# A second block of seven products per MLP, a new order of its groups, and weight loads split whole

## The chip, the cores and the metric

The kernel runs on one core of a Trainium2 chip. The metric is the device time of one execution in microseconds (us), the median of several runs; a profile is one more execution of the same program with the hardware profiler on.

The names used below: TensorE (PE, with its weight loads PEld) multiplies, VectorE (DVE) and ScalarE (ACT) work on tiles, GpSimd (POOL) does little here, and SyncE (SP) issues nearly all the transfers. Each engine takes its own instructions strictly in order and waits on semaphores for those of the others.

## The reference, cut to what matters

The input is 256 tokens by 1024 channels, in float32, and there are two layers. Each has a token mixer and then an MLP:

```python
def _conv_ffn(xn, w_up, conv_w, conv_b, w_down):      # D_FF = 2816
    a, gval = jnp.split(xn @ w_up, 2, axis=-1)
    a = depthwise_conv_of_width_3(a, conv_w) + conv_b
    return (jax.nn.gelu(a) * gval) @ w_down

for layer in range(2):
    h = h + _token_mixer(_rmsnorm(h, norm1[layer]), ...)   # w_in, pooling, attention with rel_bias, w_o
    h = h + _conv_ffn(_rmsnorm(h, norm2[layer]), ...)
return _rmsnorm(h, norm_f)
```

The attention adds to its scores a bias per head that depends on the distance of two tokens.

## The kernel before, in words

**Loads and pieces.** Every weight is read as float32 in loads of 1 MB (128 partitions of 2048 columns), into three buffers called raw. TensorE multiplies in a shorter format, so each weight is split into a high part wh, a cast by ScalarE (L259), and a low part wl, the rest raw - wh, by VectorE (L261). A product is then three passes: wh by the high part of the activations, wl by the high part, wh by the low part. A load is split in two pieces of 1024 columns, each with its own cast and difference, into five buffers for wh and five for wl. `W.get` (class Weights) is called when TensorE's matmuls of a piece are written down, and writes down the splits of the pieces up to four further on; so the order of the program is also the order of the splits on ScalarE and VectorE. A piece that comes free lets a later split begin, and a raw buffer that comes free lets SP issue a later load.

**Steps between the splits.** Other work of VectorE and ScalarE is put between the cast and the difference of a split (the list `W.between`), or behind a piece's matmuls.

**The MLP's up projection.** It is made in groups of 512 columns: ("a", n) of the branch a, ("g", n) of the branch gval, for n from 0 to 4, and ("b", 20), 256 columns of either. A group is two loads, four pieces of 12 matmuls each (`by_tokens`, L798), with tokens on the partitions. A group's sums go to channels on the partitions by a crossing: VectorE transposes (L852) two banks into a tile called crossing, SP writes 512 KB of it to memory (L857), and SP reads it back in four transfers of 128 KB (L864) into zg, zga or zb. These reads are held back until SP has issued the next load (`bring_back`), and they wait for the write to land.

**A block of seven products.** ("w", 3) makes the groups a3 and g3 together. The four quadrants 11, 12, 21, 22 of both groups' weights, and seven sums of them, are multiplied as in Strassen's method: 11, T1, 22, T2, 21, T3, T4, where the T's are sums of quadrants made by VectorE in the raw tiles (L344). Each is two half products of 6 matmuls (`products`, L917). The two plain groups would need 16 half products, the block needs 14. Copies by ScalarE (L1681, L1685, L1688) and adds by VectorE (L1692) bring the seven sums together: a "kept" sum for a, the banks p and q for g. Both go through a crossing. The attention part has one more block of this kind in each layer, for the values (the table VALUES).

**Pairs of steps.** The activated columns are made in eleven pairs (`steps_up`, f = 0, 2, ... 20). Each pair is: six fetches by ScalarE (L1602, L1604), two neighbour adds by VectorE (L1608, L1609), the gelu by ScalarE (L1612), the gate by VectorE (L1616), the cast actq by ScalarE (L1624) and the difference actk by VectorE (L1625). The table PAIR_PLACES says at which place each happens: a place is one piece or half product of the MLP, numbered from 4 pieces a group, and `at_place` (L1640) puts a pair's neighbours and gate between the splits of its place, and the fetch, gelu and the two keeps behind it.

**The down projection.** ("d", 8) and so on are the groups of w_down's rows (`residual_mm`, L715 to L717), of which the first pieces stand between the half products of the block (the "d" in the table BLOCK).

**The bias.** bt holds the bias of four heads, read once by five transfers on SP (L559).

Of the kernel before, what the change touches and what calls it, by code (L numbers as in the profile page):

```python
# [47 lines left out]
PAIR_PLACES = (  # L48
    (11, 14), (14, 16), (19, 22), (21, 23), (46, 48), (49, 51), (52, 54), (55, 57), (60, 62), (63, 65), (58, 60),
# [3 lines left out]
    ("11", 0), ("11", 1), "d", ("T1", 0), ("T1", 1), "d", "d", ("22", 0), ("22", 1), "d", ("T2", 0), ("T2", 1), "d",  # L53
    ("21", 0), ("21", 1), "d", ("T3", 0), ("T3", 1), "d", "d", ("T4", 0), ("T4", 1),
# [64 lines left out]
class Weights:  # L119
# [6 lines left out]
    RAW, BUFS, LOOK = 3, 5, 3  # L126

    def __init__(self, tc, pool, idle, small):
        self.tc, self.nc, self.pool, self.idle, self.small = tc, tc.nc, pool, idle, small
        self.loads, self.pieces = [], []  # L130
        self.n_loaded, self.n_split, self.n_got = 0, 0, 0
        self.raw, self.split = {}, {}
        self.live = set()
        self.behind, self.later = (), []
        self.last, self.rests = [None, None], {}
        self.between = []
# [3 lines left out]
        self.sums = {}  # L140

    def add(self, src, shape, cuts, tag=None):

        n = len(self.loads)
        self.loads.append((src, shape, tag))
        return [(n, cut, c_shape) for cut, c_shape in cuts]
# [61 lines left out]
    def _split(self, upto):  # L208
        nc = self.nc
        first = self.n_split  # L210
        while self.n_split < len(self.pieces):
            i = self.n_split
            n, cut, shape, slot = self.pieces[i]
            if i >= upto and (slot is None or i >= max(upto, first + 2) or i >= upto + 4 or i < 4):
                break
            if slot is None and len(self.live) == self.BUFS:
                break
            self.load(n + 1)
            with ExitStack() as queued:
                for insts, some in self.later:  # L220
                    for inst in insts if i in some else ():
                        if not self.by_hand:
                            queued.enter_context(self.tc.issue_after(inst.ins))
                for hi, lo, *_ in self.open_next():
                    hi()
                    self.run_between()
                    lo()
                if i in self.sums:
                    self.sums.pop(i)()
            self.load(self.ahead(i))  # L230

    def run_between(self):

        while self.between:
            self.between.pop(0)()

    def open_next(self):
# [3 lines left out]
        n, cut, shape, slot = self.pieces[i]  # L241
        if slot is None:
            self.live.add(i)
            h, l = (
                self.pool.tile([P, *shape], F32R, tag=tag, bufs=self.BUFS, name=f"{tag}{i}")
                for tag in ("wh", "wl")
            )
# [44 lines left out]
    def free(self, i):  # L292
        self.live.discard(i)


@with_exitstack
def encoder(ctx, tc, x, w_in, w_pool, pool_scale, w_a, w_b, w_o, norm1, norm2, w_up, conv_w,
# [32 lines left out]
    def use_block(units, made, first):  # L330
# [9 lines left out]
        def sum_later(i, name, j):  # L340

            def make():
                one, other = terms[name]
                nc.vector.tensor_sub(out=raw(name, j), in0=raw(one, j), in1=raw(other, j))  # L344

            W.sums[i] = make

        for j in range(2):
            sum_later(len(W.pieces) + first + j, "T1", j)
        behind = [u for u in units if len(u) > 2]  # L350
        for unit in units:
            if len(unit) > 2:
                W.use([unit])
                behind = behind[1:] or behind
                continue
            name, j = unit
            if name in SUMS:
                sum_later(len(W.pieces), SUMS[name], j)
            if name in ("22", "21"):
                W.use([made[name][j]])  # L360
            else:
                W.use([(behind[0][0], lambda t, name=name, j=j: raw(name, j), (2, 512))])

    def first_quadrants(w, n):
        return {
            "11": quadrant(w, 0, DFF + n * 512, "ybig"), "12": quadrant(w, 0, n * 512, "at2"),
        }

    def block(w, down, n, made):
        made = dict(made)  # L370
        d = rows(down, 0) + rows(down, 2 * P)
        made["22"] = quadrant(w, 1, n * 512)
        d += rows(down, 4 * P)
        made["21"] = quadrant(w, 1, DFF + n * 512)
        d += rows(down, 6 * P)
        d = iter(d)
        use_block([next(d) if unit == "d" else unit for unit in BLOCK], made, -2)
# [36 lines left out]
    for l in range(DEPTH):  # L414
# [24 lines left out]
        for kind, n in MLP_GROUPS:  # L439
            if (kind, n) == ("a", 2):  # L440
                corner = first_quadrants(w_up[l], 3)
            if kind == "w":
                block(w_up[l], w_down[l], n, corner)
            elif kind == "b":
                for j in range(2):
                    W.use(of_both(w_up[l], j * 512, n * P))
            elif kind == "d":
                for f in range(n, min(n + 4, NF), 2):
                    W.use(rows(w_down[l], f * P))
            else:  # L450
                for j in range(2):
                    W.use(rows(w_up[l], j * 512, 4, (kind == "g") * DFF + n * 512, 512))
# [74 lines left out]
    bt = const.tile([P, HPG, NT * P], F32, name="bt")  # L527

    def build_bias():
# [25 lines left out]
        nc.sync.dma_start(out=fd[0].rearrange("(h e) -> h e", h=HPG), in_=fsb)  # L555
        yield
        for blk, kind in enumerate((4, 3, 1, 0, 2)):
            src = bass.AP(fd.tensor, fd.offset + kind * 256, [[1, P], [NT * 256, HPG], [1, P]])
            nc.sync.dma_start(out=bt[:, :, blk * P : (blk + 1) * P], in_=src)  # L559
        yield  # L560

    def bias_of(t, hh):

        b = bt[:, hh]
# [556 lines left out]
    for l in range(DEPTH):  # L1121
# [203 lines left out]
        if l == 0:  # L1325
            visits["u", 1, 0] = visits["u", 1, 2] = ((next, bias),)

# [76 lines left out]
        def keep_gated(n):  # L1404
# [14 lines left out]
            4: ((W.bring_back,), (scores, 1)),  # L1419
# [21 lines left out]
        with tc.manual_schedule():  # L1441
# [16 lines left out]
            for kind, n in GROUPS:  # L1458
                if l and (kind, n) not in VALUES and not z_of.get(("k", 2)):
                    kz, q = keys_and_queries()  # L1460
                ps = None
                for unit in VALUES.get((kind, n), range(4)) if l else range(4):
                    if not isinstance(unit, int):
                        name, j = unit
                        products_of(name, j)
                        if j:
                            W.between.append(after[name])
# [77 lines left out]
        run(attended)  # L1545


        g1 = gain(norm1[l + 1] if l + 1 < DEPTH else norm_f)
# [82 lines left out]
        between, behind = {}, {}  # L1631
# [8 lines left out]
        def at_place(p, make, *first):  # L1640
            W.between = [*first, *(step for _, _, step in sorted(between.pop(p, ()), key=lambda x: x[:2]))]
# [24 lines left out]
        def block_units(n):  # L1666
# [3 lines left out]
                x2, s_of_x, lambda: mmp.tile([P, 512], F32, tag="mm", name="t_ps")  # L1670
            )

# [10 lines left out]
            def keep_fifth():  # L1683
                kept["m"] = big.tile([P, 2, 512], F32, tag="gates", name="kept")
# [10 lines left out]
            after = {  # L1695
                "11": (keep_first,), "T1": (keep_fifth,), "22": (keep_both,), "T2": (lambda: add(0),),
                "T3": (lambda: add(1),), "T4": (lambda: turn("g", 0, bank("p")), lambda: turn("g", 1, bank("q"))),
            }
            for unit in BLOCK:
                if unit == "d":  # L1700
                    yield lambda: next(down), ()
                else:
                    name, j = unit
                    yield lambda: products(name, j), after.get(name, ()) if j else ()
        with tc.manual_schedule():
            W.by_hand = 1
            place, turn = 8, ()
            for kind, n in MLP_GROUPS[1:]:
                ps = None
                if kind == "w":  # L1710
                    for make, after in block_units(n):
                        at_place(place, make, *turn)
                        place, turn = place + 1, after
                    continue
                for i in range(4):
                    if not between and not behind:
                        break
                    if kind == "d":
                        at_place(place, lambda: next(down), *turn)
                    else:  # L1720
                        ps = at_place(place, lambda: by_tokens(x2, 4, ps=ps, begin=i, end=i + 1), *turn)
                    turn = ()
                    place += 1
                if kind != "d":
                    turn = (lambda ps=ps, kind=kind, n=n: to_z(ps, kind, n),)
# [41 lines left out]
```

## Time and profile before

| | |
|---|---|
| time, median of 3 runs | 847.55 us (847.19 to 847.85) |
| the profiled execution | 848.11 us, of which the span is 846.3 us |
| granted TensorE clock, mean | 0.999 |
| ScalarE busy | 531.1 us, 63% of the span |
| share of the chain that ended last: PE, DMA, DVE, ACT | 90%, 3%, 3%, 2% |
| bytes moved | 214.02 MB, mean 253 GB/s |
| casts of 128x1024 by ScalarE (L259, wh) | 292, mean 1048 ns |
| differences of 128x1024 by VectorE (L261, wl) | 292, mean 1219 ns |

The first lines of a profile's page give busy time of each engine. A table of windows gives it for a stretch of the span. A timeline gives single instructions, as start, duration, engine, line and operation, tiles, and in brackets the idle time before it and who ended it. Waits are by engine: who waited, for which instruction, how long in all, how often, and the longest.

### The profile page before, as it was taken

How to read it: one execution, taken by the hardware profiler on the slowest of the kernel's cores; microseconds unless marked ns; L12 is line 12 of the kernel's file. 1: busy time of each engine (PE TensorE's matmuls, PEld its weight loads, DVE VectorE, ACT ScalarE, POOL GpSimd, SP SyncE). 2: the span in 40 equal slices, each digit the busy share in tenths (PEclk: the TensorE clock that was granted, in tenths of full speed). 3: DMA queues.
4: the chain of work that ended last, by engine and by line, in shares of the span. 5: the costliest groups of instructions: out<-in, count | busy, mean ns of one | idle time of the engine just before them, and what ended most of it. 6: DMA issues, size and time to landing. Idle time of an engine off the chain costs nothing.

```text
span 846.3 us, 10959 instructions
## 1 busy us (share of the span) xinstructions
PE 838.7 (99%) x3889; PEld 699.3 (83%) x3889; DVE 665.5 (79%) x860; ACT 531.1 (63%) x770; POOL 35.5 (4%) x96
## 2 busy tenths in 40 slices
PE   9999999999999999999999999999999999999997
PEld 7888888888888887888888888888888888888886
DVE  6968877757767799788898997868577867998884
ACT  7744556655554776488765555577455647757883
POOL 1720000000010000000000000000000100000000
PEclk9999999999999999999999999999999999999999
DMA  8699987796759886889857669968777499768861
GB/s 305 211 304 289 317 282 251 246 282 218 233 206 302 276 275 199 256 264 316 272 185 225 222 225 316 284 235 261 247 261 269 164 308 309 227 224 275 303 218 50
DMA packets 147967, 214.02 MB, mean 253 GB/s; under 512 B 7801, under 2 KB 69185, under 8 KB 147913
## 3 DMA queue, kind: packets, MB, share of 16 engines
q1 hardware_dynamic: 147480, 212.67, 76.8%
q10 hardware_dynamic: 432, 0.66, 0.2%
q8 instruction: 30, 0.49, 0.2%
q14 instruction: 25, 0.20, 0.1%
HBM read 186.02 MB, written 27.28 MB: 252 GB/s over the span
## 4 chain that ended last, share of the span: by engine, by line
PE 90%; DMA 3%; DVE 3%; ACT 2%; issue 1%; POOL 0%; ACTq 0%; SPq 0%; DVEq 0%; POOLq 0%
PE t_ps L798 54%; PE res_ps L716 6%; PE res_ps L715 6%; PE res_ps L717 6%; PE t_ps L917 4%; PE v_ps L798 3%; DMA raw<-in_w_up_dram 3%; PE v_ps L1101 3%; PE v_ps L917 2%; PE pool_ps L702 1%; PE v_ps L1000 1%; PE o_ps L1392 1%; PE s_ps L1344 1%; ACT wh L259 1%; DVE wl L261 1%; PE s_ps L1339 1%
## 5 line engine op out<-in xcount | busy, mean ns | idle before, releaser
L261 DVE TENSOR_TENSOR wl<-raw,wh 128x1024 fp32r<-128x1024 f32 x292 | 350.9, 1219 | 92.4 <-ACT wh L259 91.7
L798 PE MATMUL t_ps<-wh,x 128*128 128x512 f32 x1280 | 401.8, 390 | 0.0
L259 ACT CAST wh<-raw 128x1024 fp32r<-128x1024 f32 x292 | 302.1, 1048 | 158.8 <-PE t_ps L798 71.2
L798 PEld LDWEIGHTS t_ps<-wh,x 128*128 128x128 f32 x1280 | 240.3, 188 | 50.0
L798 PE MATMUL t_ps<-wl,x 128*128 128x512 f32 x640 | 249.0, 389 | 0.0
L798 PEld LDWEIGHTS t_ps<-wl,x 128*128 128x128 f32 x640 | 120.2, 188 | 24.7
L715 PE MATMUL res_ps<-wh,actq 128*128 128x512 f32 (+1 forms) x184 | 70.0, 380 | 0.0
L716 PE MATMUL res_ps<-wl,actq 128*128 128x512 f32 (+1 forms) x184 | 69.8, 380 | 0.0
L717 PE MATMUL res_ps<-wh,actk 128*128 128x512 f32 (+1 forms) x184 | 69.3, 380 | 0.0
L798 PE MATMUL t_ps<-wh,po 128*128 128x512 f32 x128 | 41.4, 395 | 0.0
L715 PEld LDWEIGHTS res_ps<-wh,actq 128*128 128x128 f32 x184 | 34.6, 188 | 6.7
L716 PEld LDWEIGHTS res_ps<-wl,actq 128*128 128x128 f32 x184 | 34.6, 188 | 6.7
L717 PEld LDWEIGHTS res_ps<-wh,actk 128*128 128x128 f32 x184 | 34.6, 188 | 6.5
L1604 ACT ACTIVATE a<-zga,prm 128x256 f32<-128x256 f32 x80 | 38.9, 512 | 0.0
L592 POOL TENSOR_SCALAR ss<-ss 128x1 f32<-128x1 f32 x8 | 3.1, 386 | 764.2 <-ACT junk L585 764.2
L344 DVE TENSOR_TENSOR raw<-raw,raw 128x1024 f32<-128x1024 f32 x24 | 29.3, 1222 | 0.0
L798 PEld LDWEIGHTS t_ps<-wh,po 128*128 128x128 f32 x128 | 24.0, 188 | 4.9
L715 PE MATMUL res_ps<-wh,m 128*128 128x512 f32 (+1 forms) x72 | 26.5, 368 | 0.0
L716 PE MATMUL res_ps<-wl,m 128*128 128x512 f32 (+1 forms) x72 | 26.3, 365 | 0.0
L717 PE MATMUL res_ps<-wh,m 128*128 128x512 f32 (+1 forms) x72 | 26.0, 365 | 0.0
L1608 DVE TENSOR_TENSOR y<-y,a 128x510 f32<-128x510 f32 x22 | 14.9, 679 | 13.6 <-ACT y L1602 13.6
L798 PE MATMUL t_ps<-wl,po 128*128 128x512 f32 x64 | 24.9, 390 | 0.0
(221 smaller groups left out, 1069.6 us busy)
## 6 DMA issues: line engine op xcount, KB each, us to landing
raw<-in_w_in_dram SPq DMA_DIRECT2D x58, 1024.0 KB
raw<-in_w_up_dram SPq DMA_DIRECT2D x40, 1024.0 KB
raw<-in_w_down_dram SPq DMA_DIRECT2D x22, 1024.0 KB
crossing<-crossing SPq DMA_DIRECT2D x22, 512.0 KB
crossing<-way SPq DMA_DIRECT2D x16, 512.0 KB
raw<-in_w_a_dram SPq DMA_DIRECT2D x8, 1024.0 KB
raw<-in_w_o_dram SPq DMA_DIRECT2D x8, 1024.0 KB
zga<-crossing SPq DMA_DIRECT2D x40, 128.0 KB
```

Source lines behind the costliest of these rows:

```text
L259: inst = nc.scalar.copy(out=h, in_=src)
L261: inst = self.rests[i] = nc.vector.tensor_sub(out=l, in0=src, in1=h.bitcast(F32))
L344: nc.vector.tensor_sub(out=raw(name, j), in0=raw(one, j), in1=raw(other, j))
L702: nc.tensor.matmul(out, w(k), x, start=(steps is first and k == 0), stop=(steps is last and k == nk - 1), skip_group_check=turns["rest"],)
L715: nc.tensor.matmul(ps, ah, wh, start=first, stop=False, skip_group_check=on)
L716: nc.tensor.matmul(ps, ah, wl, start=False, stop=False, skip_group_check=on)
L717: nc.tensor.matmul(ps, al, wh, start=False, stop=last, skip_group_check=on)
L798: nc.tensor.matmul(ps, x2[:, 2 * n + j, part, t, :], w[:, j, :], start=(n + m == 0), stop=(n == last and m == 5),)
L917: nc.tensor.matmul(ps, operands[name](part, 2 * j + c), w[:, c, :], start=(name in ("11", "T1") and j + m == 0), stop=(j == 1 and m == 5), ...
L1101: nc.tensor.matmul(ps[t], a[:, k, t, :], w[:, j, :], start=(k + m == 0), stop=(k == KD - 1 and m == 2),)
L1604: nc.scalar.mul(out=out, in_=a, mul=row(j, c))
L1608: nc.vector.tensor_add(out=y[:, :, 1:], in0=y[:, :, 1:], in1=t["a0"][:, :, : S - 1])
```

## The change

1. The MLP has two blocks of seven products, for n = 1 and n = 3. The pieces between the first block's half products are those of the groups g2 and b, those between the second's are d0 and d4. The order of groups is new, and so are the places of the pairs.
2. Where the attribute `two` is set, the two pieces of a load are split at once: one cast and one difference of 128x2048 (L296 and L297 after), and a sum of 128x2048 (L409). There are six slots for wh and six for wl in place of five, so that three pairs are held. `two` is off in a part of the attention (the groups q1 and k1 and what follows them up to the MLP) and for the last two groups of the MLP.
3. bt holds two heads; the last two are read at step 4 of the attention by five transfers on ScalarE's queue, and the first two again by SP in the second layer.
4. The kept sum of a block lies in another tile, the next layer's gain is read later (at group g4), the first block's banks are of the other PSUM pool, ScalarE's copies stand ahead of the next cast and not behind it, and both of the kept sum's transposes stand behind T3's products (`add_last`), where each stood behind its own add.

```diff
 MLP_GROUPS = (
-    ("g", 0), ("a", 1), ("g", 1), ("a", 2), ("g", 2), ("w", 3), ("b", 20), ("a", 4), ("g", 4),
-    ("d", 8), ("d", 12), ("d", 16), ("d", 20),
+    ("g", 0), ("a", 2), ("w", 1), ("a", 4), ("w", 3), ("g", 4), ("d", 8), ("d", 12), ("d", 16), ("d", 20),
 )
+BETWEEN = {1: (("g", 2), ("b", 4 * NQ)), 3: (("d", 0), ("d", 4))}
...
 BLOCK = (
-    ("11", 0), ("11", 1), "d", ("T1", 0), ("T1", 1), "d", "d", ("22", 0), ("22", 1), "d", ("T2", 0), ("T2", 1), "d",
-    ("21", 0), ("21", 1), "d", ("T3", 0), ("T3", 1), "d", "d", ("T4", 0), ("T4", 1),
+    ("11", 0), ("11", 1), "d", "d", ("T1", 0), ("T1", 1), "d", "d", ("22", 0), ("22", 1), "d", "d",
+    ("T2", 0), ("T2", 1), "d", "d", ("T3", 0), ("T3", 1), ("21", 0), ("21", 1), ("T4", 0), ("T4", 1),
 )
...
-    RAW, BUFS, LOOK = 3, 5, 3
+    RAW, SLOTS, LOOK = 3, 6, 3
...
+            count = 1
+            if self.makes_two(i):
+                if self.two_slots() is not None:
+                    count = 2
+                elif i >= self.n_got + 2:
+                    break
...
+                def both(n):
+                    if n == 0:
+                        return nc.scalar.copy(out=h, in_=src)
+                    inst = nc.vector.tensor_sub(out=l, in0=src, in1=h.bitcast(F32))
...
-    bt = const.tile([P, HPG, NT * P], F32, name="bt")
+    bt = const.tile([P, 2, NT * P], F32, name="bt")
...
-            4: ((W.bring_back,), (scores, 1)),
+            4: ((W.bring_back,), (scores, 1), (load_bias, 2, nc.scalar)),
...
-                turn("a", t, m)
+
+            def add_last():
+                add(1)
+                for t in range(2):
+                    turn("a", t, kept["m"][:, t])
...
+            def make():
+                sums_of[kind, n] = by_tokens(x2, 4, ps=sums_of.get((kind, n)), begin=i, end=i + 1)
```

In the whole program TensorE has 3795 matmuls after and 3819 before; VectorE's differences of 128x1024 go from 292 to 98, with 103 of 128x2048, and ScalarE's casts likewise.

Two places show what the new order is. The first is VectorE around T3 and T4, where a block ends, in the first layer. Before (the only block), raw60 holds the quadrant 21 and raw59, raw61 rows of w_down, raw50 and raw51 the sums; every split has its own wl tile:

```order
L261 TENSOR_TENSOR wl118_3032<-raw59_2940,wh118_3031 128x1024
L261 TENSOR_TENSOR wl119_3042<-raw60_3004,wh119_3041 128x1024
L344 TENSOR_TENSOR raw51_2537<-raw60_3004,raw51_2537 128x1024
L261 TENSOR_TENSOR wl120_3060<-raw60_3004,wh120_3059 128x1024
L344 TENSOR_TENSOR raw51_2537<-raw60_3004,raw51_2537 128x1024
L261 TENSOR_TENSOR wl121_3071<-raw59_2940,wh121_3070 128x1024
L1692 TENSOR_TENSOR kept_2984<-t_ps_2937,kept_2984 128x512
L852 STREAM_TRANSPOSE crossing_3084<-kept_2984 128x4x4x32
L261 TENSOR_TENSOR wl122_3081<-raw50_2535,wh122_3080 128x1024
```

After, at the block n = 1; raw47 is T3, raw55 the quadrant 21, raw49 T4, and wl_76 holds all the slots:

```order
L297 TENSOR_TENSOR wl_76<-raw54_2481,wh_75 128x2048
L1691 TENSOR_TENSOR y_2571<-y_2571,a0_2570 128x2x255
L1692 TENSOR_TENSOR y_2571<-y_2571,a2_2572 128x2x255
L297 TENSOR_TENSOR wl_76<-raw47_2259,wh_75 128x2048
L1699 TENSOR_TENSOR g_2608<-y_2571,zg_2204 128x512
L1708 TENSOR_TENSOR actk1_2252<-g_2608,actq1_2250 128x512
L1778 TENSOR_TENSOR kept_2497<-v_ps_2446,kept_2497 128x512
L297 TENSOR_TENSOR wl_76<-raw55_2501,wh_75 128x2048
L409 TENSOR_TENSOR raw49_2277<-raw55_2501,raw49_2277 128x2048
L1691 TENSOR_TENSOR y_2629<-y_2629,a0_2628 128x2x255
L1692 TENSOR_TENSOR y_2629<-y_2629,a2_2630 128x2x255
```

The neighbours (L1691, L1692), the gate (L1699) and the kept difference (L1708) of pairs now stand between a block's splits, where before there were only splits, sums and the block's own adds and transposes.

The second place is SP behind a block, in the first layer. Before, behind the only block: raw60 to raw65 are loads, and crossing_3166 is the write of the kept sum.

```order
L178 DMA raw60_3004<-in_w_up_dram 128x4x512
L178 DMA raw61_3006<-in_w_down_dram 128x2x1024
L176 DMA raw62_3087<-in_w_up_dram 128x4x256 x2
L176 DMA raw63_3090<-in_w_up_dram 128x4x256 x2
L857 DMA crossing_3166<-crossing_3084 128x2x512
L178 DMA raw64_3169<-in_w_up_dram 128x4x512
L864 DMA zga_2380<-crossing_3166 32x8x128 x4
L178 DMA raw65_3207<-in_w_up_dram 128x4x512
```

After, behind the block n = 1: crossing_2657 is the write of group b's sums, crossing_2681 that of the kept sum, raw56 and raw58 the two loads of group a4, raw57 and raw59 corners of the second block.

```order
L184 DMA raw56_2535<-in_w_up_dram 128x4x512
L945 DMA zg_2204<-crossing_2531 32x8x128 x4
L938 DMA crossing_2657<-crossing_2654 128x2x512
L938 DMA crossing_2681<-crossing_2678 128x2x512
L184 DMA raw57_2684<-in_w_up_dram 128x4x512
L945 DMA zga_2205<-crossing_2681 32x8x128 x4
L945 DMA zb_2653<-crossing_2657 32x8x128 x4
L184 DMA raw58_2694<-in_w_up_dram 128x4x512
```

Two loads stood ahead of the write before and one between the write and its reads; now two writes follow each other, one load stands behind them, and the second load of a4 comes after eight reads.

More of the change, by code (lines that the diff above doesn't have):

```diff
@@ L140, in __init__ @@
         self.sums = {}
+        self.slots = [pool.tile([P, self.SLOTS, 1024], F32R, tag=tag, name=tag) for tag in ("wh", "wl")]
+        self.freed = {slot: slot - self.SLOTS for slot in range(self.SLOTS)}
+        self.slot_of, self.n_freed = {}, 0
     def add(self, src, shape, cuts, tag=None):
@@ L338, in raw, with whole, sum_later @@
             return W.raw[made[name][0][0]][:, 2 * j : 2 * j + 2]
[L340 removed]
+        def whole(name):
+            return W.raw[made[name][0][0]]
+        def sum_later(i, name):
             def make():
                 one, other = terms[name]
[L344 removed]
+                nc.vector.tensor_sub(out=whole(name), in0=whole(one), in1=whole(other))
             W.sums[i] = make
[L348 to L349 removed]
+        sum_later(len(W.pieces) + first + 1, "T1")
         behind = [u for u in units if len(u) > 2]
@@ L1669, in block_units @@
             bank, products = halves_of_block(
-                x2, s_of_x, lambda: mmp.tile([P, 512], F32, tag="mm", name="t_ps")
+                x2, s_of_x, v_tile if n == 1 else lambda: mmp.tile([P, 512], F32, tag="mm", name="t_ps")
             )
+            between = iter([(*group, i) for group in BETWEEN[n] for i in range(4)])
             def turn(kind, t, rows):
@@ L1708, in encoder @@
             for kind, n in MLP_GROUPS[1:]:
[L1709 to L1715, printed above, removed]
+                W.two = (kind, n) not in MLP_GROUPS[-2:]
+                if (kind, n) == ("g", 4):
+                    g1 = gain(norm1[l + 1] if l + 1 < DEPTH else norm_f)
+                units = block_units(n) if kind == "w" else (piece_of(kind, n, i) for i in range(4))
+                for make, after in units:
                     if not between and not behind:
                         break
[L1718 to L1725, printed above, removed]
+                    at_place(place, make, *turn)
+                    place, turn = place + 1, after
             if l + 1 == DEPTH:
```

160 lines of the change are left out of this document (110 added, 50 removed), and 10 rows, old and new, of the table VALUES.

## The prediction

> **What bounds the kernel now.** I read the page's first line, then the table of windows, then the waits of PE, then the chain. The first line gives busy time and share of the span for each engine:
>
> ```profile
> PE 838.7 (99%) x3889; PEld 699.3 (83%) x3889; DVE 665.5 (79%) x860; ACT 531.1 (63%) x770; POOL 35.5 (4%) x96
> ```
>
> TensorE is busy 838.7 of 846.3 us, so a removed matmul is worth its whole duration as long as its operands come in time. The windows (length, then busy time of PE, PEld, DVE, ACT, POOL, then the granted clock) show how thin that condition is. The first two are the only MLP block of seven products, once in each layer; the third is the end of the program:
>
> ```profile
> 320.00:340.00 20.00, 20.00 (x90) 16.57 (x89) 19.97 (x19) 12.54 (x14) 0.00 (x0) 1.00 0.64 210
> 730.00:750.00 20.00, 20.00 (x89) 16.25 (x88) 20.00 (x21) 13.69 (x17) 0.00 (x0) 1.00 0.65 215
> 842.00:846.30 4.30, 0.00 (x0) 0.00 (x0) 0.41 (x2) 0.38 (x1) 0.00 (x0) 0.89 0.36 122
> ```
>
> In the block VectorE is busy 19.97 and 20.00 of 20 us: 79% over the span, but everything here. TensorE hardly waits in the whole program (us in total, times, longest):
>
> ```profile
> PE warm_ps L502 <- PEq L1749: 0.8, 1, 0.8
> PE t_ps L917 <- DVE crossing L852: 0.4, 1, 0.4
> PE xt_ps L627 <- DVE xn L618: 0.3, 1, 0.3
> ```
>
> So VectorE just keeps up where products stand in the MLP. The change takes work from TensorE and puts more of VectorE's work among products; the question is whether that edge is crossed.
>
> **What is removed.** A second block of seven products per layer does 14 half products of 6 matmuls in place of 16, so 12 matmuls fewer per layer; the order has 24 fewer over the program. Two pieces of the chain (start, us, what) give their price:
>
> ```profile
> 443.74 1.36 PE v_ps L917 x6
> 445.10 2.72 PE t_ps L798 x12
> ```
>
> 12 matmuls take 2.72 us: 0.2267 us each, 2.72 us a layer, 5.44 us in all. That is the whole gain on TensorE. A pair of half products takes 2 x 1.36 = 2.72 us; a pair of pieces of 12 (any other 1 MB load) 5.44 us.
>
> **Splitting both pieces at once.** VectorE's timeline (start, us, operation) around line 261 of before:
>
> ```profile
> 720.78 1.31 DVE L852 STREAM_TRANSPOSE crossing<-t_ps 128x512 f32<-128x512 f32 x2
> 722.01 0.65 DVE L1608 TENSOR_TENSOR y<-y,a 128x510 f32<-128x510 f32 x1
> 722.77 0.69 DVE L1609 TENSOR_TENSOR y<-y,a 128x510 f32<-128x510 f32 x1
> 723.37 1.22 DVE L261 TENSOR_TENSOR wl<-raw,wh 128x1024 fp32r<-128x1024 f32 x1
> ...
> 729.85 0.69 DVE L1625 TENSOR_TENSOR actk<-g,actq 128x512 fp32r<-128x512 f32 x1
> 730.45 0.69 DVE L1616 TENSOR_TENSOR g<-y,zg 128x512 f32<-128x512 f32 x1
> 731.05 1.22 DVE L261 TENSOR_TENSOR wl<-raw,wh 128x1024 fp32r<-128x1024 f32 x1
> ...
> 747.60 2.37 DVE L261 TENSOR_TENSOR wl<-raw,wh 128x1024 fp32r<-128x1024 f32 x2
> 749.87 1.23 DVE L344 TENSOR_TENSOR raw<-raw,raw 128x1024 f32<-128x1024 f32 x1
> ```
>
> Two of 1024 columns take 749.87 - 747.60 = 2.27 us from start to start, 1.135 each; those of 512 are 0.60 apart (729.85, 730.45, 731.05). So 512 columns more cost 0.53, and one of 2048 should hold the engine 1.135 + 2 x 0.53 = 2.20 us and end 2.28 us after its start. That saves 0.07 us a pair, next to nothing, and delays the first piece: the first half product can no longer start after half of the work. The other steps: transposes 722.01 - 720.78 = 1.23; the two neighbour adds 723.37 - 722.01 = 1.36; gate, kept product and add 0.60 each. ScalarE's timeline:
>
> ```profile
> 717.05 0.53 ACT L1604 ACTIVATE a<-zga,prm 128x256 f32<-128x256 f32 x1
> ...
> 719.67 1.04 ACT L259 CAST wh<-raw 128x1024 fp32r<-128x1024 f32 x1
> 723.49 0.64 ACT L1612 ACTIVATE y<-y 128x512 f32<-128x512 f32 x1 [2.77 <-DVE y L1609]
> 724.03 1.04 ACT L259 CAST wh<-raw 128x1024 fp32r<-128x1024 f32 x1
> ...
> 731.17 0.62 ACT L1624 CAST actq<-g 128x512 fp32r<-128x512 f32 x1 [0.56 <-DVE g L1616]
> 731.70 2.94 ACT L259 CAST wh<-raw 128x1024 fp32r<-128x1024 f32 x3
> ...
> 747.38 1.06 ACT L259 CAST wh<-raw 128x1024 fp32r<-128x1024 f32 x1 [2.73 <-DMA raw<-in_w_up_dram]
> ```
>
> Casts of 1024 are (2.94 - 1.04) / 2 = 0.95 us apart, those of 512 0.53 (731.17 to 731.70): one of 2048 ends after about 1.04 + 2 x 0.42 = 1.9 us. Six fetches take 719.67 - 717.05 = 2.62; a gelu 0.64, an actq 0.62. The row at 723.49 shows the coupling that matters below: ScalarE stood idle 2.77 us for VectorE, with the next cast queued behind the gelu.
>
> **A: steps among the products.** In the new order the steps of two pairs (gate, keep, neighbours, gelu) stand inside the block n = 1. Each engine takes its work in order, so gate, actq, next cast, next difference become a chain. From the end of T1's difference to that of b's second load: gate 0.6, actq 0.62, copy of a bank 0.6 (a 512-column step of ScalarE), cast 1.9, difference of g2's second load 2.2: 5.9; gate 0.6, actq 0.62, cast 1.9, difference and sum of 22 4.4: 7.5; difference of b's first load, transposes, difference and sum of T2, difference of b's second load, 4 x 2.2 + 1.23: 10.0. Together 23.4 us. TensorE's own pace over the same pieces is 2.72 + 5.44 + 2.72 + 5.44 + 2.72 = 19.04. From there to T4: neighbours 1.36, gelu 0.63, cast 1.9, difference 2.2 (T3), gate 0.6, actq 0.62, cast 1.9, difference and sum 4.4 (21), neighbours 1.36, gelu 0.63, cast 1.9, difference 2.2: 19.7 us, where TensorE takes 5.44 + 2 x 2.72 = 10.88. Together 43.2 against 29.9: 13.3 us behind. The lead at T1 can pay some of it. There are three pair slots, so T1's is free 2.72 + 5.44 = 8.16 us before T1 is due; less 1.9 + 2.28 that leaves 3.9 at most, 2.3 where VectorE is as full as the windows show. T4 comes 9.4 to 11.0 us late; I take 9.4.
>
> **B: the queue of loads behind the block.** SP's issues of before (SPq: start, us, what):
>
> ```profile
> 712.04 0.38 SPq L857 DMA_DIRECT2D crossing<-crossing  x1
> ...
> 716.40 1.80 SPq L864 DMA_DIRECT2D zg<-crossing  x4
> ...
> 722.12 0.38 SPq L857 DMA_DIRECT2D crossing<-crossing  x1
> ...
> 725.72 1.80 SPq L864 DMA_DIRECT2D zga<-crossing  x4
> ...
> 734.13 0.38 SPq L857 DMA_DIRECT2D crossing<-crossing  x1
> ...
> 736.87 1.94 SPq L864 DMA_DIRECT2D zg<-crossing  x4
> 742.08 0.39 SPq L178 DMA_DIRECT2D raw<-in_w_up_dram  x1
> ```
>
> A write of 512 KB to its first read takes 2.7 to 4.4 us (734.13 to 736.87, 712.04 to 716.40), four reads 1.8, and the 1 MB load issued at 742.08 let the cast at 747.38 go: 5.3 us. In the new order the second load of group a4 (raw58) stands on SP behind two crossing writes and eight reads, and the second write needs the kept sum, whose add and transposes follow the gate and keep after T4's difference. So raw58 is split 0.6 + 0.62 + 0.6 + 0.6 + 1.23 = 3.7 (to the transposes), + 2.7 to 4.4, + 3.6 (eight reads), + 5.3, + 1.9 + 2.28 = 19.5 to 21.2 us after T4. TensorE needs it after T4 and a4's first load, 2.72 + 5.44 = 8.16 us. It waits 11.4 to 13.0 us more; I take 11.4. Behind the blocked writes also stands raw57, the first corner of the second block, used later still. The Trainium skill (DMA: Bandwidth & Descriptors, Anatomy of one DMA) fits a transfer as about 2.0 us fixed and bytes over 436 GB/s, on GpSimd's path: 4.4 us by this estimate for 1 MB; the trace has 5.3 from SP, and with 4.4 the sum would be 1.8 us less over both layers.
>
> **C: the second block and the tail.** The kept sum's write stands ahead of g4's second load (raw67), this time without reads between: 0.6 + 1.23 + 0.4 + 5.3 + 4.2 = 11.7 us after T4's difference against 8.16, so 3.6 late, 2.4 if that difference leads by the 1.2 that its slot allows (free 5.44 us before, less 4.2). The last five pairs of steps in twelve places may cost 0 to 5 more. I take 3 of the 2.4 to 8.7, near the lower end, because before's block ran at 20.00 of 20 us of VectorE without a wait of PE.
>
> **What costs nothing, with its cover.** The bias of the last two heads is five issues on ScalarE's queue; before's five on SP:
>
> ```profile
> L559 SPq DMA_DIRECT2D bt<-fd x5: 366/508/2216, 48.9 to 51.2; - x5
> ```
>
> 5 x 0.37 to 0.51 = 1.8 to 2.5 us of delay for the casts behind, covered by the split pieces ahead (ScalarE is 63% busy); uncovered it is 5 us in two layers. Moving the kept tile and the gain load frees or fills nothing on TensorE: 0. The attention part's block, now split in pairs, saves 0.07 us a pair on VectorE and may lose 0 to 2 us for the later first half: I take 0, as its groups of 12 matmuls cover it.
>
> **The sum.** Per layer 9.4 + 11.4 + 3 - 2.72 = 21.1; twice 42.2. The profiled execution took 848.11 us (span 846.3, 0.56 over the median of 847.55), so it would become 890.3, and the median 889.7: 890. High end: 2 x (11.0 + 13.0 + 8 - 2.72) = 58.6, 906.
>
> **The rivals.** (1) Other side: TensorE stays the bound. The walk of A takes every hand-over at its full length; if leads of three pairs and idle stretches of ScalarE absorb A and raw58 comes before its turn, only the matmuls count: 847.55 - 5.44 = 842.1. It decides if VectorE is never over 8.16 us behind its slots' release and raw58 is issued 8 us before T4. For it: before does this at the edge with 20.00 of 20. Against: raw58's place in SP's order. (2) B alone: T4 comes in time, but the kept add still needs T3's matmuls, which end at 35.36 us of the block's own pace; a4's second load is due at 46.24 and ready at 35.36 + 1.83 + 2.7 to 4.4 + 3.6 + 5.3 + 4.2 = 53.0 to 54.7, about 7.6 late: 2 x (7.6 - 2.72) = 9.8, 857, or 862 with C. (3) A alone, the load issued in time: 2 x (9.4 - 2.72) = 13.4 to 2 x (11.0 + 3 - 2.72) = 22.6: 861 to 870. (4) No change: a layer's loss of just 2.72. (5) Slower clock after the pauses. The trace grants 1.00 in the block and 0.89 only where 4.3 us have no matmul; four pauses of 9 to 13 us, each costing up to one product pair and a piece pair at half rate, 8.16 us, would add up to 33 us. The Trainium skill (TensorE: Matmul & The Clock Gate, HAM oscillation) says that gaps of over about 3.4 us throttle TensorE to half for some 1.67 us: an estimate of 3 us for four pauses, still inside the range; before's longest wait of 0.8 us cannot show it.
>
> **How the numbers follow.** A and B together, 880 to 906 (A may be 5 where hand-overs overlap: 2 x (5 + 11.4 + 2.4 - 2.72) = 32): 0.66. B alone 0.09, A alone 0.08, TensorE the bound 0.10, no change 0.03, over 906 by the clock 0.04. A range from 857 to 906 leaves 0.17 out. 0.2% (1.7 us) is about what a measurement of this kernel tells from no change: faster 0.10, same 0.03, slower 0.87.
>
> **What would show it.** In the profile after: PE's waits near 49 us (2 x 23.8 and before's 1.5) in place of 1.5, in two or three places per layer: on differences of line 297 at T2 to T4, and once on a4's second load, with SP's issue of it right behind eight reads; matmuls of line 798 and 917 at the same pace; VectorE with gaps released by ScalarE's cast in block 1. If PE shows no waits there and a4's second load is issued before T4, A and B are wrong and the time is near 842.

## The result, and the profile after

The changed kernel takes 940.4 us (median of 4 runs, 939.29 to 943.6) against 847.7: 1.110 times as long, 95% interval 1.107 to 1.113. The forecast was 890, with a range up to 906. Slower was right; the loss is 93 us where 42 were expected.

The page of after, busy time of each engine, from an execution of 939.29 us with a span of 936.8:

```profile
PE 862.1 (92%) x3865; PEld 706.5 (75%) x3865; DVE 690.3 (74%) x769; ACT 529.1 (56%) x685; POOL 35.4 (4%) x96
```

The span grew by 936.8 - 846.3 = 90.5 us. TensorE's idle time went from 7.6 to 74.7 us, 67.1 more. Its busy time rose by 23.4, though 5.4 us of matmuls are gone: 28.8 us more for the others. By its timeline some 17 us of that are in about 80 matmuls at half pace; most of the rest lies in the matmul before and the one behind each stop. The waits of PE in after name the places (us in total, times, longest):

```profile
PE t_ps L879 <- ACT wh L296: 21.0, 5, 8.5
PE v_ps L998 <- DVE kept L1778: 19.0, 4, 6.6
PE t_ps L879 <- DVE wl L297: 10.2, 7, 1.8
PE res_ps L797 <- DVE wl L297: 7.4, 6, 1.8
PE xt_ps L708 <- DVE xn L699: 4.5, 2, 3.6
PE t_ps L998 <- DVE kept L1778: 2.6, 2, 1.3
```

They are in the MLP. Up to 260 us of the span TensorE is busy 257.80 us after and 259.15 before; in the rest of the first layer it is busy 180.57 of 215 us where before it was 172.29 of 173 (windows of after, then of before; busy PE is the second number):

```profile
0.00:260.00 260.00, 257.80 (x1218) 215.17 (x1219) 189.19 (x265) 146.81 (x207) 26.84 (x77) 1.00 0.79 256
260.00:475.00 215.00, 180.57 (x751) 144.41 (x750) 156.86 (x136) 123.04 (x153) 3.88 (x7) 0.93 0.67 220
```

```profile
0.00:260.00 260.00, 259.15 (x1228) 217.14 (x1229) 193.01 (x281) 151.74 (x222) 26.73 (x77) 1.00 0.80 261
260.00:433.00 173.00, 172.29 (x777) 142.16 (x775) 143.71 (x167) 120.98 (x180) 4.12 (x7) 1.00 0.83 273
```

At the end of the first layer's block n = 1, TensorE's timeline of after shows three stops: T3, T4, and a4's second load, whose first matmul waits for the cast and whose second for the difference.

```profile
319.96 0.77 PE L998 MATMUL v_ps<-wh,sx 128*128 128x512 f32 x1 [2.96 <-DVE kept L1778]
...
333.72 0.77 PE L998 MATMUL v_ps<-wh,x 128*128 128x512 f32 x1 [6.62 <-DVE kept L1778]
...
352.00 0.80 PE L879 MATMUL t_ps<-wh,x 128*128 128x512 f32 x1 [8.47 <-ACT wh L296]
354.32 0.80 PE L879 MATMUL t_ps<-wl,x 128*128 128x512 f32 x1 [1.53 <-DVE wl L297]
```

VectorE's timeline there shows why T4 stops for a "kept" add. T4 adds to the bank that the add reads, and the add stands behind T4's difference (328.70), a gate and its kept part:

```profile
328.70 2.29 DVE L297 TENSOR_TENSOR wl<-raw,wh 128x2048 fp32r<-128x2048 f32 x1 [1.26 <-ACT wh L296]
330.91 0.68 DVE L1699 TENSOR_TENSOR g<-y,zg 128x512 f32<-128x512 f32 x1
332.28 0.69 DVE L1708 TENSOR_TENSOR actk<-g,actq 128x512 fp32r<-128x512 f32 x1 [0.69 <-ACT actq L1707]
332.88 0.68 DVE L1778 TENSOR_TENSOR kept<-v_ps,kept 128x512 f32<-128x512 f32 x1
```

T4's operands were there at 331.0; the add let it start at 333.7. VectorE stood idle for 0.69 us before actk, since nothing lies between the gate and it. SP's timeline for the same place, where the corner's load (raw57) is issued at 335.24 and the second load of a4 (raw58) at 344.73:

```profile
327.47 7.72 SPq L938 DMA_DIRECT2D crossing<-crossing  x2
335.24 1.17 SPq L184 DMA_DIRECT2D raw<-in_w_up_dram  x1
337.95 1.80 SPq L945 DMA_DIRECT2D zga<-crossing  x4
339.85 4.84 SPq L945 DMA_DIRECT2D zb<-crossing  x4
344.73 1.01 SPq L184 DMA_DIRECT2D raw<-in_w_up_dram  x2
```

The chain's pieces there, from the corner's load on:

```profile
335.24 9.13 DMA raw<-in_w_up_dram
...
344.38 0.30 SPq L945
...
344.73 5.24 DMA raw<-in_w_up_dram
...
350.05 1.91 ACT wh L296
351.98 2.30 DVE wl L297
```

The load's last three steps are as forecast: 5.24 us to land, 1.91 for the cast, 2.30 for the difference. The eight reads ahead of it are not: they were out after 6.7 us (337.95 to 344.69), where the forecast had 3.6. By the chain the last of them waited until the corner's load had landed, 9.13 us after its issue.

### The profile page after: what moved, and what is told of

It is laid out like the page before. It is cut to its first block, busy times and chain, and to the rows that moved or that the text cites. A ratio compares the mean times of both kernels' runs of the same rounds, so it can differ in the third digit from the quotient of the medians.

```text
span 936.8 us, 10671 instructions
## 1 busy us (share of the span) xinstructions
PE 862.1 (92%) x3865; PEld 706.5 (75%) x3865; DVE 690.3 (74%) x769; ACT 529.1 (56%) x685; POOL 35.4 (4%) x96
## 4 chain that ended last, share of the span: by engine, by line
PE 54%; DVE 16%; ACT 12%; DMA 10%; issue 6%; SPq 1%; ACTq 0%; POOL 0%; DVEq 0%; POOLq 0%
PE t_ps L879 37%; DVE wl L297 7%; ACT wh L296 6%; DMA raw<-in_w_up_dram 4%; PE v_ps L879 4%; DVE raw L409 3%; PE v_ps L1182 2%; DMA crossing<-crossing 2%; PE v_ps L998 2%; ACT a L1687 2%; DMA raw<-in_w_down_dram 2%; PE pool_ps L783 1%; DVE g L1699 1%; PE v_ps L1081 1%; ACT y L1685 1%
## 5 line engine op out<-in xcount | busy, mean ns | idle before, releaser
L879 PE MATMUL t_ps<-wh,x 128*128 128x512 f32 x1152 | 372.0, 398 | 21.0 <-ACT wh L296 21.0
L297 DVE TENSOR_TENSOR wl<-raw,wh 128x2048 fp32r<-128x2048 f32 x103 | 235.2, 2285 | 104.6 <-ACT wh L296 101.4
L879 PEld LDWEIGHTS t_ps<-wh,x 128*128 128x128 f32 x1152 | 221.4, 192 | 69.5 <-ACT wh L296 23.2
L296 ACT CAST wh<-raw 128x2048 fp32r<-128x2048 f32 x103 | 196.0, 1907 | 134.9 <-DMA raw<-in_w_up_dram 56.1
L879 PE MATMUL t_ps<-wl,x 128*128 128x512 f32 x576 | 229.7, 399 | 10.4 <-DVE wl L297 10.2
L320 DVE TENSOR_TENSOR wl<-raw,wh 128x1024 fp32r<-128x1024 f32 x98 | 116.5, 1217 | 34.9 <-ACT wh L318 34.9
L318 ACT CAST wh<-raw 128x1024 fp32r<-128x1024 f32 x98 | 100.4, 1047 | 25.2 <-PE t_ps L879 14.1
L409 DVE TENSOR_TENSOR raw<-raw,raw 128x2048 f32<-128x2048 f32 x20 | 45.7, 2284 | 0.0
L998 PE MATMUL v_ps<-wh,sx 128*128 128x512 f32 x96 | 33.9, 416 | 5.9 <-DVE kept L1778 5.9
L998 PE MATMUL v_ps<-wh,x 128*128 128x512 f32 x72 | 26.3, 429 | 13.0 <-DVE kept L1778 13.0
```

Source lines behind the costliest of these rows:

```text
L296: return nc.scalar.copy(out=h, in_=src)
L297: inst = nc.vector.tensor_sub(out=l, in0=src, in1=h.bitcast(F32))
L318: inst = nc.scalar.copy(out=h, in_=src)
L320: inst = self.rests[i] = nc.vector.tensor_sub(out=l, in0=src, in1=h.bitcast(F32))
L409: nc.vector.tensor_sub(out=whole(name), in0=whole(one), in1=whole(other))
L879: nc.tensor.matmul(ps, x2[:, 2 * n + j, part, t, :], w[:, j, :], start=(n + m == 0), stop=(n == last and m == 5),)
```

## The experiments

Fourteen kernels ran. At the start, theory ORDER held that A and B are the loss; its rival GRAIN, that splitting a load whole is. Times are medians, to be compared with 940.4 after and 847.7 before.

**e1, pieces again** (`makes_two` is always false):

```diff
     def makes_two(self, i):
+        return False
```

> The changed kernel with every load split piece by piece again (six slots, order and places as in the change). Theory ORDER (the loss comes from where steps and loads stand in the queues: A, the pairs' steps in the first block, and B, a4's second load behind eight reads) expects little: the first half product may start about 1 us earlier at each stop, 915 to 942 us, with the waits of PE on the kept adds (L1778) and on the load behind the block still there. Theory GRAIN (splitting a load whole is what starves TensorE) expects most of the loss back: below 880 us.

914.8 us. 25.6 us back: far from the GRAIN forecast, and just past the most that ORDER allowed ("about 1 us earlier at each stop"). Both theories hold a part.

**e2, steps out of the first block:**

```diff
-    (9, 13), (11, 15), (35, 38), (41, 45), (22, 25), (26, 29), (60, 64), ...
+    (9, 13), (11, 15), (36, 40), (41, 45), (33, 36), (34, 38), (60, 64), ...
```

> The changed kernel with the steps of the pairs f = 8 and f = 10 moved from the first block behind it (places 33 to 38, where VectorE stood idle for 15 us), and f = 4 by a place or two. ORDER expects A's waits gone, 2.96 + 6.62 us per layer, and the slow matmuls behind them, some 1.6 us each: 24 to 28 us less over both layers, 911 to 918 us, with B's wait left as it is. GRAIN expects 935 to 945.

935.4 us: ORDER missed. The waits at T3 and T4 are all but gone (0.9 us at each T4), and almost nothing is won. Its waits of PE show the loss in other rows:

```profile
PE t_ps L879 <- ACT wh L296: 23.2, 5, 9.5
PE res_ps L797 <- DVE wl L297: 13.1, 11, 1.8
...
PE v_ps L998 <- DVE kept L1778: 1.9, 2, 1.0
```

**e3, a4's second load ahead of the reads:**

```diff
-            if self.by_hand == 1:
+            if self.by_hand == 1 and tag is None:
                 self.bring_back()
```

> The changed kernel with one condition more: held-back reads of a crossing are not issued behind the load of a corner, so a4's second load comes on SP right behind the corner's load and ahead of the eight reads, about 8 us earlier. ORDER expects B's wait (8.5 + 1.5 us in the first layer, 7.4 + 1.5 in the second) to shrink to 0 to 3 us and the slow matmuls behind it (3.6 and 2.7 us) with it: 918 to 926 us. GRAIN expects 935 to 945.

940.8 us: ORDER missed. The load is issued 8 us earlier (at 336.1 in place of 344.7), right behind the corner's. These are the chain's piece from its issue to its landing, then the issue of the two loads (SPq at 334.77) and SP's reads, which take longer to issue:

```profile
336.12 10.08 DMA raw<-in_w_up_dram
```

```profile
334.77 1.91 SPq L184 DMA_DIRECT2D raw<-in_w_up_dram  x2
337.69 2.34 SPq L945 DMA_DIRECT2D zga<-crossing  x4
340.07 6.45 SPq L945 DMA_DIRECT2D zb<-crossing  x4
```

It landed after 10.1 us in place of 5.2, so 4 us are won there (stop of 4.60 in place of 8.47) and lost again in the second block: at its T4 e3 is 1.3 us ahead of after, at the layer's end 0.4. That the two loads slowed each other is not shown, since in after the corner's load alone took 9.13 us at this place.

**e4, both edits:**

> Both edits together: steps out of the first block, and the load ahead of the reads. ORDER expects the two gains to add up: 890 to 900 us, what is left being the second block and the tail (about 9 us of waits per layer) and the end of the layer. GRAIN expects 935 to 945.

928.5 us: 12 us back where the two should have brought some 45. Stalls do not add up here.

For the next four a theory BLOCK was set against GRAIN (the groups and the second block are to blame, not whole splits), and CLOCK against CHAIN (do slow matmuls cost time?).

**e5, the old groups with whole splits:**

```diff
-    ("g", 0), ("a", 2), ("w", 1), ("a", 4), ("w", 3), ("g", 4), ("d", 8), ...
+    ("g", 0), ("a", 1), ("g", 1), ("a", 2), ("g", 2), ("w", 3), ("b", 20), ("a", 4), ("g", 4),
+    ("d", 8), ...
-BETWEEN = {1: (("g", 2), ("b", 4 * NQ)), 3: (("d", 0), ("d", 4))}
+BETWEEN = {3: (("d", 0), ("d", 4))}
```

and PAIR_PLACES as before.

> The changed kernel with the groups and pair places of before (one block, n = 3, with d0 and d4 between its half products in the change's BLOCK order); loads split whole, six slots, bias and the rest as changed. The first four runs showed that A's and B's stalls do not add up: taking one away lets the next come. Theory BLOCK: the second block among the MLP's groups, with the pairs' steps crowded into less room, makes the loss; splitting whole costs only what the first four runs showed, some 25 us, in company with it. It expects 848 to 860 us here. Theory GRAIN: a load split whole costs by itself, because every second place has no split between a gate and its kept parts, so VectorE and ScalarE wait for each other: 865 to 890 us.

874.2 us, as GRAIN expected.

**e6, the same with pieces:**

> As the run before it, with every load split piece by piece as well: of the change only the six slots, the bias by ScalarE's queue, the kept tile, the late gain and the order of copies and adds are left. BLOCK and GRAIN both expect 846 to 854 us; over 860 would mean that one of the small edits costs much, which the trace before the first MLP (1.3 us of PE's waits in place of 0.8) speaks against.

856.8 us, ratio 1.007 (1.003 to 1.011): 3 us over what was expected. The rest of the change (slots, bias, tiles, the block's order) costs some 7 us; which of it was not tried. With e1 and after this gives a square: pieces 857 and 915, whole 874 and 940, for the old and the new groups. The new groups cost 58 to 66 us, whole splits 17 to 26. GRAIN is right that whole splits cost by themselves, BLOCK that the groups cost most.

**e7, the pairs' steps spread by one place:**

```diff
-                (behind, p1, 2, fetch_up), (between, p1 + 1, 1, neighbours), (behind, p1 + 1, 1, activate),
-                (between, p3, 0, gate), (behind, p3, 0, keep_up),
+                (behind, p1, 2, fetch_up), (between, p1 + 1, 1, neighbours), (behind, min(p1 + 2, p3 - 1), 1, activate),
+                (between, p3, 0, gate), (behind, p3 + 1, 0, keep_up),
```

> The changed kernel with each pair's gelu one place later (where its gate leaves room) and its kept parts (actq, actk) one place behind the gate, so that a split can lie between them. GRAIN expects VectorE's 8.2 us of idle time before actk (12 times 0.69) to go, and some of its idle time behind gelus: 10 to 25 us less, 915 to 930 us. ORDER and BLOCK expect no gain, 936 to 943.

907.7 us: 33 us back by two places in a table, more than GRAIN's 10 to 25 and more than whole splits cost. VectorE's waits in after:

```profile
DVE wl L297 <- ACT wh L296: 101.4, 52, 15.0
...
DVE y L1691 <- ACT y L1685: 12.8, 6, 2.9
...
DVE actk L1708 <- ACT actq L1707: 8.2, 12, 0.7
```

and in e7, where none for actk is left:

```profile
DVE wl L297 <- ACT wh L296: 82.7, 42, 14.5
...
DVE y L1691 <- ACT y L1685: 6.2, 4, 2.0
```

**e8, three pauses filled** with matmuls of no use, into a bank that is read no more:

```diff
+                    spare = {("T3", 0): 10, ("T4", 0): 24}.get(unit, 0)
...
+                if (kind, n, i) == ("a", 4, 2):
+                    fill(banks_of[1]("t"), 32)
```

> The changed kernel with matmuls of no use (128x512, into a bank that is read no more) ahead of three waits of TensorE in each layer: 10 ahead of T3, 24 ahead of T4, 32 ahead of a4's second load, 2.3, 5.4 and 7.3 us where the trace has waits of 3.0, 6.5 and 7.4 to 8.5. Theory CLOCK: the 28.8 us by which TensorE's matmuls are slower than before come from the pauses, and those behind these three (some 7 us a layer) are time lost: 926 to 932 us. Theory CHAIN: what follows waits for VectorE, ScalarE and the loads anyway, so faster matmuls only lengthen later waits: 936 to 942. Both expect the matmuls behind the filled pauses at 0.23 us and not at 0.43.

938.4 us. Behind the fill the T4 products run at 0.23 us each in place of 0.43, in TensorE's timeline of e8:

```profile
332.79 0.47 PE L998 MATMUL v_ps<-wh,x 128*128 128x512 f32 x1 [2.61 <-DVE kept L1778]
333.10 0.39 PE L998 MATMUL v_ps<-wl,x 128*128 128x512 f32 x1
333.33 0.62 PE L998 MATMUL v_ps<-wh,x 128*128 128x512 f32 x2
333.79 0.40 PE L998 MATMUL v_ps<-wl,x 128*128 128x512 f32 x1
```

The expectation of both, full pace behind all three, held at T3 and T4 but not at a4's second load, where pauses of 1.37 and 1.83 us were left and some 3 us of slow matmuls followed. The time moved by 2 us: CLOCK missed, CHAIN held. In this kernel the slow matmuls behind T3's and T4's pauses fill time that would have been waited.

Next, HANDOVER (VectorE and ScalarE wait for each other, in fixed orders) against WORK (VectorE has too much to do).

**e9, everything eased:** e1, e2, e3 and e7 together.

> The changed kernel's two blocks and groups, with everything else eased: loads split piece by piece, gelu and kept parts spread over one place more, the steps of f = 8 and f = 10 behind the first block, a4's second load ahead of the reads. Theory HANDOVER (the loss is VectorE and ScalarE waiting for each other in their fixed orders; the runs so far: pieces -25 us, spread -33 us, steps and load -12 us) expects most of it back: 860 to 885 us, the rest being the second block's stops for its kept sum and loads. Theory WORK (with two blocks VectorE simply has too much to do beside the products) expects no less than 895.

896.2 us: 11 over what HANDOVER expected, and in WORK's range. **e10, the same with whole splits:**

> As the run before it, but with loads split whole as in the change: spread, steps behind the first block, load ahead of the reads. HANDOVER expects 885 to 900 us: the spread's 907.7 and up to 12 to 20 us less. If the edits are in each other's way as the first two were, 900 to 910.

899.5 us. With the steps spread and out of the block and the load ahead of the reads, whole splits cost 3 us in place of 26. **e11, without the sums of quadrants** (its products are of the plain quadrants; of the twenty sums four are the attention part's, which has such a block in the second layer only):

```diff
-                nc.vector.tensor_sub(out=whole(name), in0=whole(one), in1=whole(other))
+                if W.by_hand != 1:
+                    nc.vector.tensor_sub(out=whole(name), in0=whole(one), in1=whole(other))
```

> The changed kernel without the twenty sums of quadrants (L409): 16 in the two MLPs' blocks and 4 in the second layer's values, so the products are of the plain quadrants. That takes 20 x 2.2 = 44 us of work from VectorE, 17.6 in each MLP, and leaves every cast, difference, step and load where it is. WORK expects most of the MLPs' 35 us back, 905 to 915. HANDOVER expects less, as VectorE stands idle for over 100 us behind casts anyway: 918 to 932. If loads and crossings alone set the pace, 936 to 942.

922.8 us: 44 us of VectorE's work less gave 18, as HANDOVER expected. WORK missed here. What e9 still waited for were the casts of two loads, as its waits of PE show:

```profile
PE t_ps L880 <- ACT wh L319: 13.9, 4, 4.1
PE t_ps L999 <- DVE wl L321: 3.5, 2, 1.7
PE t_ps L880 <- DVE wl L321: 2.4, 4, 0.8
```

**e12, e9 with two loads earlier,** ahead of the block's crossing writes and not just ahead of their reads:

```diff
                     name, j = unit
+                    if unit == ("T3", 0):
+                        W.load(W.n_loaded + 2)
```

> The kernel of e9 (two blocks, pieces, steps spread and behind the first block) with two loads more written ahead of T3's products in both blocks, so that on SP the corner's load and a4's second load (and g4's second load) stand ahead of the block's two crossing writes. Theory LOADS (what e9 still loses, waits of 2.9 to 4.1 us on ScalarE's cast of those loads, and 2.4 to 3.3 us of slow matmuls behind each, hangs on loads queued behind writes that wait for the kept sum) expects 28 us less than e9: 863 to 873 us. WORK (too much for VectorE) expects 888 or more.

867.9 us, as LOADS expected, and well under WORK's 888: 28 us back by two lines. **e13, that edit alone on the changed kernel, and e14, e10 with it:**

> The changed kernel with nothing but that: two loads ahead of T3's products. B's and C's waits on loads should go (8.5 + 1.5 and 0.7 + 1.8 in the first layer, 7.4 + 1.5 and 4.3 + 1.5 in the second). If stalls add up: 905 to 915 us. HANDOVER expects that the steps' chain takes most of it back, as in e3: 925 to 940.

> As the first of the three, with loads split whole as in the change (the kernel of e10 with the loads early). LOADS expects 872 to 882 us, some 8 us over the first for the whole splits; WORK 890 or more.

e13 takes 920.8 us: 19.6 back, 4 more than HANDOVER allowed and 6 less than if stalls added up, so both missed. e14 takes 871.6, 0.4 us under the range of LOADS. SP's issues of both loads in e12 stand ahead of the writes, the second of which goes out only at 319.6:

```profile
308.43 0.95 SPq L184 DMA_DIRECT2D raw<-in_w_up_dram  x2
315.13 4.52 SPq L939 DMA_DIRECT2D crossing<-crossing  x2
```

and its waits of PE have no such load in them:

```profile
PE res_ps L797 <- ACT actq L1708: 4.9, 2, 2.5
PE t_ps L999 <- DVE wl L321: 3.4, 2, 1.7
PE res_ps L798 <- DVE wl L321: 3.4, 7, 0.8
```

e12 is still 1.022 times before (1.018 to 1.026). No version beat before.

## Why the prediction came out as it did

**Right: the direction and the mechanism of A and B; their price in part by luck.** First layer, A: 0.68 + 1.29 + 2.96 + 6.62 = 11.6 us of stops (9.4 to 11.0 expected); B: 8.47 + 1.53 = 10.0 (11.4 to 13.0 expected). With 11.2 and 8.9 in the second layer they make 41.7, forecast 41.6. The durations of the widths held: 2285 ns for a difference of 2048 columns (2.28 expected), 1907 for a cast (1.9). But one dependency was missed: T3 and T4 wait for the kept add, since they add to the bank that it reads, so T4 started 2.7 us behind its difference. And in B two errors cancel: a4's second load was split 23.3 us behind T4's difference (19.5 in the sum), since the reads waited for the corner's load, and TensorE came to it after 12.5 us (8.16 in the sum), since T4 started late and at half pace.

**Right: removed matmuls, bias, attention.** 24 matmuls went, and up to 260 us of the span, which covers the first layer's attention, TensorE's busy time is 1.35 us less.

**The step that failed: two small terms of the sum.** Of the 90.5 us by which the span grew 48.3 are not in the forecast's 42.2: 14.1 are C, 3.6 the first layer's end, 28.8 TensorE's longer matmuls, and the rest small waits elsewhere.

**Wrong in size: C.** It was set at 3 us per layer, "near the lower end, because before's block ran at 20.00 of 20 us of VectorE without a wait of PE". The first layer's second block waited 1.29 + 0.66 + 1.82 = 3.8 and its tail 1.76 + 0.93 + 1.31 + 1.25 = 5.3 us, together 9.0; the upper end was 8.7. In the second layer these stops make 11.1, so C is 20.1 us in place of 6. Behind it came 3.6 us at the first layer's end that no term had (xt_ps waiting for xn). The reason given was bad: no step of a pair stood in before's block, so its running without a wait says nothing of a block with steps in it.

**Wrong in size: the clock, taken as 0.** The 28.8 us of longer matmuls, some 17 of them at half pace, are most of what is missing: waits of 68 us for 49 forecast, and 29 for none. The prediction had the mechanism as a rival, with 33 us as its price and a chance of 0.04, and let an estimate of 3 us stand beside it, inside the range. The same text forecast four pauses of 9 to 13 us, so a price for them belonged in the sum. But e8 shows that this row is not a cost that can be taken away alone.

**Wrong as a picture: stalls that stand each for itself.** The sum took A, B and C as stalls on TensorE's own pace. Added up as they came, with the longer matmuls, they do make the loss; but taking one away does not give its part back. They are stalls of one chain: SP's queue, ScalarE and VectorE in fixed orders. e2, e3 and e4 took away A's or B's stall and gave 5, 0 and 12 us; the later stops took the time back. Only kernels that eased the chain at many places (e7: 33 us) or let loads run ahead of it (e12: 28 us less than e9) gave as much as the stalls removed; e13 alone gave 19.6 of the 27 us of waits that it was to remove.

**Wrong: whole splits as a saving of "0.07 us a pair, next to nothing".** The time of one instruction was right, its place was not: with a split at every second place only, a gate has no split behind it to cover actq, and VectorE waits. 17 to 26 us by e5, e6, e1 and after; 3 to 4 by e9, e10, e12 and e14, where the steps are spread. These four also carry the edits of e2 and e3, so the comparisons point at the steps without showing that they are all of it. A rival stays untested: the delay of a load's first piece, which the prediction named and gave no price. With pieces, in e1, the first layer's stop at a4's second load is 6.41 + 0.47 us in place of 8.47 + 1.53.

**Open:** the 7 us of e6, and the 11 us between e12 and e6. TensorE's waits of e12 place most of the second (4.9, 3.4 and 7.1 us on lines 797, 798 and 999), but no run parted the causes.

## What to carry to other kernels

Stalls on a chain of engines that work in fixed orders do not come off one by one, so price a change by walking the chain to its end, past the last stop, and not by the stop that it removes. Two instructions that hand to each other need other work between them in each engine's order; when a change halves the places at which such work stands, look at the pairs that it uncovers, even if the work itself gets no dearer. A load that stands on a queue behind a write which waits for a result is late by that result; put it ahead of the write, not just ahead of the write's reads.

## What the runs showed of the hardware

TensorE's matmuls ran at half pace (0.43 us each in place of 0.23) after some short pauses. In after, behind the pause of 2.96 us they did so for about 3 us; behind 6.62 us also about 3; behind 8.47 and 1.53 some 6.4, with the granted clock of these windows down to 0.57:

```profile
318.00:328.00 10.00, 7.13 (x24) 5.48 (x24) 8.30 (x8) 6.70 (x10) 0.00 (x0) 0.83 0.00 0
333.00:343.00 10.00, 9.28 (x35) 7.60 (x36) 3.95 (x4) 1.04 (x1) 0.00 (x0) 0.82 0.74 213
352.00:362.00 10.00, 8.47 (x22) 6.34 (x23) 9.90 (x8) 6.78 (x9) 0.00 (x0) 0.57 1.01 378
```

The pause of 1.29 us at 303.31 left the pace as it was. The Trainium skill (TensorE: Matmul & The Clock Gate, HAM oscillation) states that gaps of over about 3.4 us throttle TensorE; here one of 2.96 us was enough, and a pair of 0.66 and 1.82 us with one matmul between was followed by some 3 us of slow ones too. The measurement decides: shorter pauses count. But length alone does not settle it: behind a pause of 2.61 us in e8 (332.79) the matmuls ran at full pace, behind one of 2.29 us in e1 (316.66) they took 0.43 us.

One load of 1 MB landed 5.24 us after its issue (344.73 in after), another 9.13 us (335.24 in after, with eight reads of 128 KB issued behind it), and in e3 the second of two, with the same eight reads behind, 10.08 us. Those reads took 6.7 us to issue in after and 8.8 in e3, where four took 1.8 to 2.2 in the first layer of before. The profile puts 2.9 and 3.3 us of that down to waiting for a load to land; why a read would wait for one is not shown.
